# Sparse attention two heads deep: three logits tiles, mask added to the bias on GpSimd, late projections over ten heads

## The chip, the cores and the metric

One core of a Trainium2 chip. Its engines run their own queues in order and wait for each other through semaphores: TensorE (PE in the profile, its weight loads PEld) multiplies matrices into PSUM, VectorE (DVE) and ScalarE (ACT) read PSUM and SBUF, GpSimd (POOL) works on SBUF, and SyncE (SP) issues the DMAs. The metric is the device time of one execution in microseconds.

## The reference, cut to what matters

Two transformer layers over 512 tokens of width 1024. The first mixes tokens by stick-breaking attention, the second by sparse attention; after each comes a gated MLP with a short causal convolution. The change touches the second mixer alone:

```python
q = rms_norm(q.reshape(B, S, 16, 128), q_gain)      # 16 heads
k = rms_norm(lat, k_gain)                           # one shared latent key, 128 wide
isc = ...                                           # indexer scores, causal
_, sel = lax.top_k(isc, topk)                       # 128 keys kept for each query
logits = q . k[sel] * 128 ** -0.5 + rel_bias[bucket(t - sel)]
logits = where(sel <= t, logits, -1e30)
p = softmax(logits);  o = p @ lat[sel];  o = o @ w_uv   # per head
```

The kernel does not gather. It computes all causal logits and adds a mask, 0 for a kept key and -1e30 for another.

## The kernel before, in words

The order on every engine is the program's own order: the whole body is traced under a manual schedule, and tiles, buffers and semaphores are laid out by the framework. A tile name with `bufs=n` is a ring of n buffers; a new tile waits until the last reader of the old one in its buffer is done. Tags let several names share a ring.

The sparse attention (`dsa_layer`) first runs the indexer and the top-k. Under the top-k's VectorE work, eleven of the sixteen heads' queries are projected (`EARLY_Q = 11`): `project_steps` gives eight steps of three 512-column matmuls (`mm3`, high and low parts, L239 to L241). `q_hi` copies the result to `qh` and squares it into `q2`, `q_lo` forms the rest `ql`, `q_sum` sums the squares by eight tiny matmuls into PSUM tag "x", and `q_norm` turns sums into the scale `rq` (L916 to L920). Weight chunks (`raw`, six buffers, fetched by SP) are split into `whi` on ScalarE (L199) and `wlo` on VectorE (L207).

Then comes the edited part, the attention itself. A head has four query tiles j of 128 rows; tile j has (j + 1) x 128 causal keys, so a head has 1280 logits columns in a tile `L`. For each tile:

- `logits(h, j)`: on TensorE three matmuls of query parts with key parts into the PSUM tile z (tag "z", two buffers), and a fourth, L1106, that multiplies the identity with the mask `maskb` (bf16) and so adds the mask.
- `softmax(h, j)`: on VectorE L1114, z times the query's scale plus the bias, read backwards from `th`, into L; then L1116, the row maximum.
- `expo(h, j)`: on ScalarE the exponential in place (L1121), with its row sum.
- `transposed(h, pi)`: three groups of transposes of L on TensorE (4, 4 and 2 blocks, L1132; PSUM tag "tr", two buffers), each copied to `pT`.

For each pair of heads there are `pair_values` (values times latents, L1147), `weighted` (probabilities times values, sixteen matmuls, L1164), and the division by the row sums: `pair_sums` (copy `rvb`), `pair_scale` (transposes of `rvb` into `bc`), `pair_hi` and `pair_lo`. `load_bias(h)` is a DMA of 256 KB that writes the head's bias row, shifted by partition, into `th`.

In iteration h the loop transposes head h while it computes the logits of head h + 1. Four of the five late projections (heads 12 to 15) lie as filler in heads 1 to 8, four steps in each; the one of head 11 lies in the prologue, which computes head 0's logits. The last late head is finished in iteration 9, with one `q_norm(11, 16)`.

Of the kernel before, what the change touches and what calls it, by code (L numbers as in the profile page):

```python
# [9 lines left out]
F32 = mybir.dt.float32  # L10
# [8 lines left out]
D = 1024  # L19
S = 512  # L20
P = 128
# [14 lines left out]
H2 = S // 2  # L36
QRING = 12
EARLY_Q = 11
AHEAD = 2
FETCH = 1  # L40
IDXFILL = [1, 1, 1, 0, 1, 1, 1, 1]
# [74 lines left out]
def kernel_body(ctx, tc, xT, wst, cst, smalls, crow, relb, onehot, outT):  # L116
# [13 lines left out]
    def ptile(shape, name, tag):  # L130
        return banks.tile(shape, F32, name=name, tag=tag, bufs=nbanks[tag])
# [736 lines left out]
    def dsa_layer(l, first, man):  # L868
        with ExitStack() as st:
# [15 lines left out]
            def project_steps(ps, ck):  # L885
                whi, wlo = ck
                for k in range(KT):
                    w = slice(k * P, (k + 1) * P)
                    mm3(ps, whi[:, w], wlo[:, w], hs[k][0], hs[k][1], k == 0, k == KT - 1)
                    yield  # L890

            def q_hi(h, pt):
                qh = pp.tile([P, S], F32R, name="qh", bufs=QRING)
                ql = pp.tile([P, S], F32R, name="ql", bufs=QRING)
                q2 = pp.tile([P, S], F32, name="q2")
                act.activation(qh, pt, AF.Copy)
                act.activation(q2, pt, AF.Square)
                Q[h] = (qh, ql)
                Q[h, 2] = q2

# [5 lines left out]
            def q_sum(h):  # L906
                q2 = Q.pop((h, 2))
                ssq = ptile([P, QT], "ssq", "x")
                for j in range(QT):
                    pe.matmul(ssq[:, j:j + 1], lhsT=q2[:, j * P:(j + 1) * P], rhs=ones1, start=True, stop=True)  # L910
                c = slice(h * QT, (h + 1) * QT)
                act.activation(msq[:, c], ssq, AF.Copy, scale=1.0 / P)

# [159 lines left out]
            with ExitStack() as sa:  # L1073
# [2 lines left out]
                uvc = chunk_raw(("uv",)).rearrange("p (a b) -> p a b", a=HEADS)  # L1076
                ths = {}
                heads = {}
                late = {}

                def late_q(h):
                    late["h"], late["pt"] = h, ptile([P, S], "pt_q", "mm")
                    late["steps"] = project_steps(late["pt"], chunk(("dq", h), 0))

                def load_bias(h):
                    th = ths[h] = ap.tile([P, S], F32, name="th", bufs=2)
                    ov = rb[h:h + 1, 0:1]
                    nc.sync.dma_start(th, bass.AP(tensor=ov.tensor, offset=ov.offset, ap=[[1, P], [1, S]]))

                def begin(h):  # L1090
                    L = ap.tile([P, LW], F32, name="L")
                    if h % 2 == 0:
                        rv = ap.tile([P, QT, 2], F32, name="rv", bufs=4)
                        heads["rv"] = rv
                    heads[h] = (L, ap.tile([P, QT], F32, name="nm"), ap.tile([P, QT], F32, name="sum"), heads["rv"], {})

                def logits(h, j):
                    qh, ql = Q[h]
                    ns = (j + 1) * P
                    qs = slice(j * P, ns)  # L1100
                    ls = slice(LOFF[j], LOFF[j] + ns)
                    z = heads[h][4][j] = ptile([P, S], "z", "z")
                    pe.matmul(z[:, :ns], lhsT=qh[:, qs], rhs=kph[:, :ns], start=True, stop=False)
                    pe.matmul(z[:, :ns], lhsT=ql[:, qs], rhs=kph[:, :ns], start=False, stop=False)
                    pe.matmul(z[:, :ns], lhsT=qh[:, qs], rhs=kpl[:, :ns], start=False, stop=False)
                    pe.matmul(z[:, :ns], lhsT=ident_b, rhs=maskb[:, ls], start=False, stop=True)  # L1106

                def softmax(h, j):
                    L, nm, sum_, rv, z = heads[h]
                    z = z.pop(j)  # L1110
                    ns = (j + 1) * P
                    ls = slice(LOFF[j], LOFF[j] + ns)
                    c = h * QT + j
                    dve.scalar_tensor_tensor(L[:, ls], z[:, :ns], rq[:, c:c + 1], ths[h][:, :ns][:, ::-1],  # L1114
                                             op0=OP.mult, op1=OP.add)
                    dve.tensor_reduce(nm[:, j:j + 1], L[:, ls], axis=AX.X, op=OP.max, negate=True)  # L1116

# [47 lines left out]
                                          rhs=ts[e][:, c:c + n], start=i == 0, stop=pi == 2)  # L1165

                def pair_sums(rv):
                    rvb = ap.tile([P, QT, 2, 64], F32, name="rvb", tag="bs")
                    dve.tensor_copy(rvb, rv[:, :, :, None].to_broadcast([P, QT, 2, 64]))
                    return rvb  # L1170

                pair = {}
# [1 line left out]
                def pair_scale(rvb):  # L1174

                    bc = ptile([P, S], "bc", "x")
                    for j in range(QT):
                        pe.transpose(bc[:, j * P:(j + 1) * P], rvb[:, j].rearrange("p a b -> p (a b)"), ident)
                    bs = pair["bs"] = ap.tile([P, S], F32, name="bs")
                    act.activation(bs, bc, AF.Copy)  # L1180

                def pair_hi():
# [7 lines left out]
                def pair_lo():  # L1190
                    dve.tensor_sub(O[-1][1], pair["bs"], O[-1][0].bitcast(F32))

                load_bias(0)
                load_bias(1)
                begin(0)
                late_q(EARLY_Q)
                for j in range(QT):
                    logits(0, j)
                    drain(late["steps"], 2)
                    softmax(0, j)  # L1200
                    expo(0, j)
                    if j == 1:
                        split_hi()
                q_hi(late["h"], late["pt"])
                for h in range(HEADS):
                    n = h + 1
                    more = n < HEADS
                    filling = 1 <= h <= 2 * (HEADS - EARLY_Q - 1)
                    after = h > 1 and h % 2 and late["h"]
                    values = h % 2 == 0 and h > 0  # L1210
                    if more:
                        begin(n)
                        for j in range(2):
                            logits(n, j)
                        softmax(n, 0)
                        expo(n, 0)
                    if values:
                        weighted(h - 2)
                    transposed(h, 0, True)
                    if more:  # L1220
                        softmax(n, 1)
                        expo(n, 1)
                    if h == 0 or after:
                        q_lo(late["h"], late["pt"])
                    if after:
                        split_hi()
                        done = late["h"]
                        if not filling:
                            q_sum(done)
                    if h % 2 and h > 1:  # L1230
                        pair_lo()
                    if filling:
                        if h % 2:
                            late_q(EARLY_Q + 1 + h // 2)
                        drain(late["steps"], 2)
                    if more:
                        logits(n, 2)
                        softmax(n, 2)
                        expo(n, 2)
                    dve.reciprocal(heads[h][3][:, :, h % 2], heads[h][2])  # L1240
                    if values:
                        rvb = pair_sums(heads[h - 1][3])
                    transposed(h, 1, False)
                    if more:
                        logits(n, 3)
                    if h % 2:
                        pair_values(h - 1)
                    transposed(h, 2, True)
                    if values:
                        pair_scale(rvb)  # L1250
                    if more:
                        softmax(n, 3)
                        expo(n, 3)
                        if n + 1 < HEADS:
                            load_bias(n + 1)
                    if h == 0:
                        split_lo()
                    if h == 1:
                        split_hi()
                        split_lo()  # L1260
                        q_sum(EARLY_Q)
                    if after:
                        split_lo()
                        if filling:
                            q_sum(done)
                        else:
                            q_norm(EARLY_Q, HEADS)
                            late["h"] = None
                    if filling:
                        drain(late["steps"], 2)  # L1270
                        if h % 2 == 0:
                            q_hi(late["h"], late["pt"])
                    if values:
                        pair_hi()
                pair_scale(pair_sums(heads[HEADS - 1][3]))
# [113 lines left out]
```

## Time and profile before

| what | value |
|---|---|
| median of 3 runs | 1334.76 us (1333.66 to 1335.91) |
| profiled execution | 1335.43 us, its span 1333.7 us |
| mean granted clock of TensorE | 0.992 of 2.4 GHz |
| busy, share of the span | PE 96%, DVE 72%, ACT 44%, POOL 2% |
| attention part that is edited | 779.70 to 917.37 us of the span |

The span goes from the first instruction to the last; the run's time has a little around it. Busy shares are averages over stages with different limits, and a busy PE is not PE at its peak, since matmuls are pipelined and their ends are modelled. What a stage is worth is read from the stage itself: by stretch, by waits, and by the start times of neighbours on one queue.

### The profile page before, as it was taken

Reading aid. Unit: us, or ns where it says so; the run is one execution under the profiler, and the core shown is the slowest. Engines: PE = TensorE matmul, PEld = TensorE weight load, DVE = VectorE, ACT = ScalarE, POOL = GpSimd, SP = SyncE. Lnnn points to the kernel's source line nnn. Section 1 sums busy time; section 2 is a strip of 40 time slices with the busy share of each in tenths; the row PEclk is TensorE's granted clock in tenths of the full one; section 3 lists DMA queues with packets and bytes.
Section 4 is the critical chain, followed back from the end, with each engine's and each line's share of the span. In section 5 each row is a group of like instructions: output and inputs, shape, how many; then the busy total and the mean of one; then the engine's idle time right before and its main releaser. Section 6 shows DMA issues by size and latency. Waiting matters only on the chain.

```text
span 1333.7 us, 17868 instructions
## 1 busy us (share of the span) xinstructions
PE 1283.2 (96%) x6900; PEld 1069.2 (80%) x6900; DVE 960.9 (72%) x1570; ACT 592.3 (44%) x1051; POOL 22.9 (2%) x22
## 2 busy tenths in 40 slices
PE   2899999999999999999999999989999999999998
PEld 0688878799888888888988877766998888888888
DVE  6987988877877877875778986685676546556653
ACT  4575666454423323443554345573454324324430
POOL 3200000000000000000100000000000000000000
PEclk8999999999999999999999999999999999999999
DMA  7624343423566575554212211112222332333221
GB/s 276 242 82 159 117 146 121 143 75 103 182 227 199 179 244 192 190 180 153 77 51 79 79 48 61 59 41 110 72 87 76 114 105 77 108 106 95 72 87 64
DMA packets 49894, 162.69 MB, mean 122 GB/s; under 512 B 5601, under 2 KB 7905, under 8 KB 49810
## 3 DMA queue, kind: packets, MB, share of 16 engines
q1 hardware_dynamic: 49810, 161.56, 37.5%
q8 instruction: 54, 0.88, 0.3%
q14 instruction: 30, 0.25, 0.1%
HBM read 159.40 MB, written 2.14 MB: 121 GB/s over the span
## 4 chain that ended last, share of the span: by engine, by line
PE 89%; DVE 7%; ACT 2%; issue 1%; DMA 1%; SPq 0%; DVEq 0%; ACTq 0%
PE pt_u L240 11%; PE pt_u L239 11%; PE pt_u L241 11%; PE pt_d L240 5%; PE pt_d L241 5%; PE pt_d L239 5%; PE pt_q L239 2%; PE pt_q L241 2%; PE pt_q L240 2%; PE pt_l L239 2%; PE pt_l L240 2%; PE pt_l L241 2%; PE pt_first L241 2%; PE pt_first L239 2%; PE pt_qk L239 2%; PE pt_first L240 2%
## 5 line engine op out<-in xcount | busy, mean ns | idle before, releaser
L199 ACT ACTIVATE whi<-raw 128x1024 fp32r<-128x1024 f32 (+1 forms) x206 | 205.0, 1002 | 141.2 <-PE pt_d L241 102.6
L207 DVE TENSOR_TENSOR wlo<-raw,whi 128x1024 fp32r<-128x1024 f32 (+1 forms) x206 | 240.1, 1168 | 17.0 <-ACT whi L199 15.9
L240 PE MATMUL pt_u<-hhi,wlo 128*128 128x512 f32 x640 | 249.2, 389 | 0.0
L241 PE MATMUL pt_u<-hlo,whi 128*128 128x512 f32 x640 | 249.2, 389 | 0.0
L239 PE MATMUL pt_u<-hhi,whi 128*128 128x512 f32 x640 | 249.2, 389 | 0.0
L806 ACT ACTIVATE y<-pt_u,sm 128x512 f32<-128x512 f32 x80 | 62.1, 776 | 190.9 <-PE pt_u L241 190.9
L239 PEld LDWEIGHTS pt_u<-hhi,whi 128*128 128x128 f32 x640 | 120.1, 188 | 25.1
L241 PEld LDWEIGHTS pt_u<-hlo,whi 128*128 128x128 f32 x640 | 120.2, 188 | 24.8
L240 PEld LDWEIGHTS pt_u<-hhi,wlo 128*128 128x128 f32 x640 | 120.2, 188 | 24.7
L807 DVE SCALAR_TENSOR_TENSOR y<-pt_u,sm,y 128x511 f32<-128x511 f32 x80 | 59.9, 749 | 98.3 <-ACT y L806 98.3
L248 DVE SCALAR_TENSOR_TENSOR raw<-raw,cond 128x1024 f32<-128x1024 f32 x96 | 120.0, 1261 | 0.0
L241 PE MATMUL pt_d<-actlo,whi 128*128 128x512 f32 x288 | 112.2, 389 | 0.0
L239 PE MATMUL pt_d<-acthi,whi 128*128 128x512 f32 x288 | 112.1, 389 | 0.0
L240 PE MATMUL pt_d<-acthi,wlo 128*128 128x512 f32 x288 | 112.1, 389 | 0.0
L350 DVE SCALAR_TENSOR_TENSOR x<-pt_d,mod,x 128x512 f32<-128x512 f32 x48 | 36.0, 750 | 72.8 <-PE pt_d L241 72.8
L239 PE MATMUL pt_first<-hhi,whi 128*128 128x256 f32 (+1 forms) x224 | 69.4, 310 | 7.6 <-ACT hhi L532 7.6
L241 PE MATMUL pt_first<-hlo,whi 128*128 128x256 f32 (+1 forms) x224 | 68.8, 307 | 8.2 <-DVE hlo L535 7.9
L223 ACT ACTIVATE acthi<-y 128x512 fp32r<-128x512 f32 x44 | 27.8, 632 | 104.3 <-DVE y L825 104.3
L240 PE MATMUL pt_first<-hhi,wlo 128*128 128x256 f32 (+1 forms) x224 | 67.9, 303 | 0.0
L239 PEld LDWEIGHTS pt_d<-acthi,whi 128*128 128x128 f32 x288 | 54.1, 188 | 11.3
L240 PEld LDWEIGHTS pt_d<-acthi,wlo 128*128 128x128 f32 x288 | 54.1, 188 | 11.2
L241 PEld LDWEIGHTS pt_d<-actlo,whi 128*128 128x128 f32 x288 | 54.1, 188 | 11.2
(228 smaller groups left out, 2647.2 us busy)
## 6 DMA issues: line engine op xcount, KB each, us to landing
raw<-wst SPq DMA_DIRECT2D x255, 512.0 KB, 3.7
raw<-wst SPq DMA_DIRECT2D x48, 384.0 KB, 2.9
th<-rb SPq DMA_DIRECT2D x16, 256.0 KB, 3.2
x<-xT SPq DMA_DIRECT2D x8, 256.0 KB, 5.6
outT<-x SPq DMA_DIRECT2D x16, 128.0 KB, 1.7
sm<-smalls SPq DMA_DIRECT2D x1, 248.0 KB, 2.7
cons<-cst SPq DMA_DIRECT2D x1, 192.0 KB, 5.4
oh<-onehot SPq DMA_DIRECT2D x1, 80.0 KB, 1.8
```

The source lines that it names most:

```text
L199: act.activation(hi[:, :n], raw[:, :n], AF.Copy)
L207: dve.tensor_sub(lo[:, :n], raw[:, :n], hi[:, :n].bitcast(F32))
L223: act.activation(hi, src, AF.Copy)
L239: pe.matmul(out, lhsT=whi, rhs=ahi, start=start, stop=False)
L240: pe.matmul(out, lhsT=wlo, rhs=ahi, start=False, stop=False)
L241: pe.matmul(out, lhsT=whi, rhs=alo, start=False, stop=stop)
L248: dve.scalar_tensor_tensor(raw, raw, 1.0, cond, op0=OP.mult, op1=OP.mult, accum_out=dst)
L350: dve.scalar_tensor_tensor(x[f][:, c], pt, mod[l][:, g * KT + f:g * KT + f + 1], x[f][:, c], op0=OP.mult, op1=OP.add)
L806: act.activation(y, pt, AF.Identity, scale=cw[2], bias=sm[:, b + S_CB + c:b + S_CB + c + 1])
L807: dve.scalar_tensor_tensor(y[:, 1:], pt[:, :S - 1], cw[1], y[:, 1:], op0=OP.mult, op1=OP.add)
```

## The change

The mask no longer goes through TensorE: L1106 is removed, and `begin(h)` adds bias (read backwards) and mask into L on GpSimd, four adds a head. `softmax` then adds L to the scaled logits in place. There are three L tiles, and the loop works two heads ahead: iteration h transposes head h and computes the logits of head h + 2; the prologue computes heads 0 and 1. The adds for head h + 3 and the bias load for head h + 4 stand at the end of iteration h. `th` goes from two buffers to one; heads 1 and 2 take buffers of the weight ring.

The late projections are issued through `late_steps(n)`: two steps at each of the prologue's eight tiles, then one step at two places of every iteration and at a third place of every even one, until head 15 is done; that is 16 steps in the prologue and 24 in iterations 0 to 9. They are normalized in two groups, `q_norm(11, 14)` and `q_norm(14, 16)`.

To make room, `q2` and `rvb` become two half-size tiles each in rings of the norm (`ln`, `sqt`), written by two instructions for one; `bs` has one buffer. Within an iteration `weighted` and the first group of transposes now stand ahead of the second logits tile, and the second group of transposes ahead of the third.

```diff
...
 EARLY_Q = 11
+LATE_NORM = 14
...
         def q_hi(h, pt):
-        q2 = pp.tile([P, S], F32, name="q2")
+        q2 = [npool.tile([P, H2], F32, name="q2", tag="ln", bufs=2) for _ in range(2)]
         act.activation(qh, pt, AF.Copy)
-        act.activation(q2, pt, AF.Square)
+        for i in range(2):
+            act.activation(q2[i], pt[:, halves[i]], AF.Square)
...
         for j in range(QT):
-            pe.matmul(ssq[:, j:j + 1], lhsT=q2[:, j * P:(j + 1) * P], rhs=ones1, start=True, stop=True)
+            pe.matmul(ssq[:, j:j + 1], lhsT=q2[j // 2][:, j % 2 * P:j % 2 * P + P], rhs=ones1, start=True, stop=True)
...
         heads = {}
-        late = {}
-
-        def late_q(h):
-            late["h"], late["pt"] = h, ptile([P, S], "pt_q", "mm")
-            late["steps"] = project_steps(late["pt"], chunk(("dq", h), 0))
+        late = {"h": EARLY_Q, "k": 0, "done": []}
+
+        def late_steps(n):
+
+            for _ in range(n):
+                h = late["h"]
+                if h == HEADS:
+                    return
+                if late["k"] == 0:
+                    late["pt"] = ptile([P, S], "pt_q", "mm")
+                    late["steps"] = project_steps(late["pt"], chunk(("dq", h), 0))
+                next(late["steps"])
+                late["k"] += 1
+                if late["k"] == KT:
+                    drain(late["steps"])
+                    q_hi(h, late["pt"])
+                    late["done"].append((h, late["pt"]))
+                    late["k"] = 0
+                    late["h"] += 1
         def load_bias(h):
-            th = ths[h] = ap.tile([P, S], F32, name="th", bufs=2)
+            if h in (1, 2):
+                th = ths[h] = raws.tile([P, D], F32, name="th", tag="raw")[:, :S]
+            else:
+                th = ths[h] = ap.tile([P, S], F32, name="th", bufs=1)
             ov = rb[h:h + 1, 0:1]
             nc.sync.dma_start(th, bass.AP(tensor=ov.tensor, offset=ov.offset, ap=[[1, P], [1, S]]))
         def begin(h):
-            L = ap.tile([P, LW], F32, name="L")
+            L = ap.tile([P, LW], F32, name="L", bufs=3)
             if h % 2 == 0:
                 rv = ap.tile([P, QT, 2], F32, name="rv", bufs=4)
                 heads["rv"] = rv
-            heads[h] = (L, ap.tile([P, QT], F32, name="nm"), ap.tile([P, QT], F32, name="sum"), heads["rv"], {})
+            for j in range(QT):
+                ls = slice(LOFF[j], LOFF[j] + (j + 1) * P)
+                pool.tensor_add(L[:, ls], ths[h][:, :(j + 1) * P][:, ::-1], maskb[:, ls])
+            heads[h] = (L, ap.tile([P, QT], F32, name="nm", bufs=3), ap.tile([P, QT], F32, name="sum", bufs=3), heads["rv"], {})
...
         def logits(h, j):
-            ls = slice(LOFF[j], LOFF[j] + ns)
             z = heads[h][4][j] = ptile([P, S], "z", "z")
             pe.matmul(z[:, :ns], lhsT=qh[:, qs], rhs=kph[:, :ns], start=True, stop=False)
             pe.matmul(z[:, :ns], lhsT=ql[:, qs], rhs=kph[:, :ns], start=False, stop=False)
-            pe.matmul(z[:, :ns], lhsT=qh[:, qs], rhs=kpl[:, :ns], start=False, stop=False)
-            pe.matmul(z[:, :ns], lhsT=ident_b, rhs=maskb[:, ls], start=False, stop=True)
+            pe.matmul(z[:, :ns], lhsT=qh[:, qs], rhs=kpl[:, :ns], start=False, stop=True)
...
         def softmax(h, j):
-            dve.scalar_tensor_tensor(L[:, ls], z[:, :ns], rq[:, c:c + 1], ths[h][:, :ns][:, ::-1],
+            dve.scalar_tensor_tensor(L[:, ls], z[:, :ns], rq[:, c:c + 1], L[:, ls],
...
         def pair_sums(rv):
-            rvb = ap.tile([P, QT, 2, 64], F32, name="rvb", tag="bs")
-            dve.tensor_copy(rvb, rv[:, :, :, None].to_broadcast([P, QT, 2, 64]))
+            rvb = [npool.tile([P, H2], F32, name="rvb", tag="sqt", bufs=3) for _ in range(2)]
+            for i in range(2):
+                dve.tensor_copy(rvb[i].rearrange("p (a b c) -> p a b c", a=2, b=2),
+                                rv[:, 2 * i:2 * i + 2, :, None].to_broadcast([P, 2, 2, 64]))
...
             for j in range(QT):
-                pe.transpose(bc[:, j * P:(j + 1) * P], rvb[:, j].rearrange("p a b -> p (a b)"), ident)
-            bs = pair["bs"] = ap.tile([P, S], F32, name="bs")
+                pe.transpose(bc[:, j * P:(j + 1) * P], rvb[j // 2][:, j % 2 * P:j % 2 * P + P], ident)
+            bs = pair["bs"] = ap.tile([P, S], F32, name="bs", bufs=1)
...
-        load_bias(0)
-        load_bias(1)
-        begin(0)
-        late_q(EARLY_Q)
-        for j in range(QT):
-            logits(0, j)
-            drain(late["steps"], 2)
-            softmax(0, j)
-            expo(0, j)
-            if j == 1:
-                split_hi()
-        q_hi(late["h"], late["pt"])
+        for h in range(3):
+            load_bias(h)
+        for h in range(3):
+            begin(h)
+        load_bias(3)
+        for h in range(2):
+            for j in range(QT):
+                logits(h, j)
+                late_steps(2)
+                softmax(h, j)
+                expo(h, j)
+                if j == 1:
+                    split_hi()
+                if j == 2:
+                    split_lo()
+                if h == 1 and j == 0:
+                    q_lo(*late["done"][0])
+                if h == 1 and j == 2:
+                    q_sum(late["done"].pop(0)[0])
         for h in range(HEADS):
-            n = h + 1
+            n = h + 2
             more = n < HEADS
-            filling = 1 <= h <= 2 * (HEADS - EARLY_Q - 1)
-            after = h > 1 and h % 2 and late["h"]
             values = h % 2 == 0 and h > 0
+            done = late["done"].pop() if late["done"] else None
             if more:
-                begin(n)
-                for j in range(2):
-                    logits(n, j)
-                softmax(n, 0)
-                expo(n, 0)
+                logits(n, 0)
+            late_steps(1)
...
             if more:
+                softmax(n, 0)
+                expo(n, 0)
+                logits(n, 1)
                 softmax(n, 1)
                 expo(n, 1)
-            if h == 0 or after:
-                q_lo(late["h"], late["pt"])
-            if after:
+            if done:
+                q_lo(*done)
                 split_hi()
-                done = late["h"]
-                if not filling:
-                    q_sum(done)
             if h % 2 and h > 1:
                 pair_lo()
-            if filling:
-                if h % 2:
-                    late_q(EARLY_Q + 1 + h // 2)
-                drain(late["steps"], 2)
+            transposed(h, 1, False)
+            late_steps(1)
...
                 rvb = pair_sums(heads[h - 1][3])
-            transposed(h, 1, False)
+            transposed(h, 2, True)
...
                 pair_values(h - 1)
-            transposed(h, 2, True)
             if values:
                 pair_scale(rvb)
+            if done:
+                q_sum(done[0])
             if more:
                 softmax(n, 3)
                 expo(n, 3)
-                if n + 1 < HEADS:
-                    load_bias(n + 1)
-            if h == 0:
+            if done:
                 split_lo()
-            if h == 1:
-                split_hi()
-                split_lo()
-                q_sum(EARLY_Q)
-            if after:
-                split_lo()
-                if filling:
-                    q_sum(done)
-                else:
-                    q_norm(EARLY_Q, HEADS)
-                    late["h"] = None
-            if filling:
-                drain(late["steps"], 2)
-                if h % 2 == 0:
-                    q_hi(late["h"], late["pt"])
+                if done[0] == LATE_NORM - 1:
+                    q_norm(EARLY_Q, LATE_NORM)
+                elif done[0] == HEADS - 1:
+                    q_norm(LATE_NORM, HEADS)
+            if h + 3 < HEADS:
+                begin(h + 3)
+            if h + 4 < HEADS:
+                load_bias(h + 4)
+            if h % 2 == 0:
+                late_steps(1)
             if values:
                 pair_hi()
         pair_scale(pair_sums(heads[HEADS - 1][3]))
```

## Rows read from the trace of the kernel before

**Rows 1.** The profile's page: busy us, share of the span, instructions.

```profile
PE 1283.2 (96%) x6900; PEld 1069.2 (80%) x6900; DVE 960.9 (72%) x1570; ACT 592.3 (44%) x1051; POOL 22.9 (2%) x22
```

**Rows 2.** Stretch and length; PE, PEld, DVE, ACT, POOL busy; PEclk, DMA, GB/s.

```profile
779.70:789.41 9.71, 9.71 (x42) 7.76 (x42) 6.27 (x15) 5.59 (x12) 0.00 (x0) 0.82 0.18 57
844.62:863.20 18.58, 17.94 (x114) 13.83 (x114) 12.42 (x25) 10.35 (x28) 0.00 (x0) 1.00 0.19 56
893.11:906.19 13.08, 11.89 (x82) 8.51 (x82) 10.51 (x23) 8.08 (x24) 0.00 (x0) 1.00 0.52 180
779.70:917.37 137.67, 127.43 (x803) 95.79 (x802) 97.19 (x204) 82.24 (x220) 0.00 (x0) 0.99 0.22 70
```

**Rows 3.** Waits, 775 to 925 us: us in total, times, longest.

```profile
DVE L L1114 <- PE z L1106: 29.5, 17, 4.0
...
PE ssq L910 <- ACT vals L1151: 2.1, 4, 0.5
```

**Rows 4.** Timeline of DVE: start, us, what, idle time before it.

```profile
901.21 0.55 DVE L1116 TENSOR_REDUCE nm<-L 128x1 f32<-128x384 f32 x1
...
901.77 0.66 DVE L1139 COPY pT<-tr 128x512 f32<-128x512 f32 x1
902.34 0.74 DVE L1114 SCALAR_TENSOR_TENSOR L<-z,cols,th 128x512 f32<-128x512 f32 x1
...
904.30 0.47 DVE L1114 SCALAR_TENSOR_TENSOR L<-z,cols,th 128x256 f32<-128x256 f32 x1
...
907.51 0.62 DVE L1114 SCALAR_TENSOR_TENSOR L<-z,cols,th 128x384 f32<-128x384 f32 x1 [2.28 <-PE z L1106]
```

**Rows 5.** Timeline of PE around a first and second logits tile.

```profile
813.99 0.23 PE L1106 MATMUL z<-maskb,ident_b 128*128 128x128 bf16 x1
814.02 0.36 PE L1103 MATMUL z<-kph,qh 128*128 128x256 f32 x1
```

**Rows 6.** Timeline of PE in the late heads and at the end.

```profile
886.54 0.34 PE L1106 MATMUL z<-maskb,ident_b 128*128 128x384 bf16 x1
886.72 0.60 PE L1132 MATMUL tr<-cons,L 128*128 128x128 f32 x4
...
887.86 0.39 PE L1106 MATMUL z<-maskb,ident_b 128*128 128x512 bf16 x1
888.08 1.05 PE L1147 MATMUL pv<-raw,latf 128*128 128x128 f32 x8
...
890.74 2.38 PE L1164 MATMUL av<-pT,vals 128*64 128x512 f32 x16
893.04 0.66 PE L1132 MATMUL tr<-cons,L 128*128 128x128 f32 x4
893.45 0.42 PE L1103 MATMUL z<-kph,qh 128*128 128x384 f32 x1
...
912.00 0.77 PE L1132 MATMUL tr<-cons,L 128*128 128x128 f32 x5 [1.68 <-ACT L L1121]
```

**Rows 7.** Timeline of all engines around the late norm.

```profile
875.83 0.69 DVE L1116 TENSOR_REDUCE nm<-L 128x1 f32<-128x512 f32 x1
...
876.44 1.21 DVE L207 TENSOR_TENSOR wlo<-raw,whi 128x1024 fp32r<-128x1024 f32 x1
...
877.39 1.28 ACT L916 ACT_TABLE_LOAD   x1
...
879.95 0.35 DVE L1114 SCALAR_TENSOR_TENSOR L<-z,cols,th 128x128 f32<-128x128 f32 x1
```

**Rows 8.** Line L525 on POOL: count, duration ns min/median/max, first and last start.

```profile
L525 POOL TENSOR_TENSOR xr<-x,r x8: 1260/2238/2253, 22.0 to 35.8; 128x512 f32<-128x512 f32 x8
```

**Rows 9.** Timeline of DVE in the first layer's start.

```profile
36.88 2.28 DVE L248 SCALAR_TENSOR_TENSOR raw<-raw,cond 128x1024 f32<-128x1024 f32 x1
...
39.90 1.21 DVE L248 SCALAR_TENSOR_TENSOR raw<-raw,cond 128x1024 f32<-128x1024 f32 x1
```

**Rows 10.** Tile th: its DMAs from issue to landing.

```profile
DMA to landing us min/median/max: 3.0/3.2/4.6
```


## Prediction

> **What bounds the kernel now.** I read the profile from the outside in. The page first: TensorE (PE) is busy 96% of the span and GpSimd (POOL) 2% [rows 1], so what shortens PE's own queue can pay, and what relieves another engine pays only where PE waits for it. Then busy time by stretch: the edited attention runs from 779.70 to 917.37 us, 137.67 us with PE busy 127.43, and it has two regimes [rows 2]. While late query projections fill PE (the pair of heads at 844.62) a pair takes 18.58 us, PE 17.94 of it, VectorE (DVE) 12.42: PE sets the pace. Behind the last projection (893.11) a pair takes 13.08 us with DVE busy 10.51. The waits say who is late: DVE sits 29.5 us before the softmax's first step (L1114) for the logits tile z, released by the mask matmul L1106 [rows 3]. In the late regime one wait is typical: 2.28 us at the third tile [rows 4], whose logits stand on PE behind `weighted`. Without it DVE's work in such a pair is 13.08 - 2.28 = 10.8.
>
> **The sum's base.** The profiled execution took 1335.43 us (span 1333.7 plus 1.7 around it); the median of the three runs, 1334.76, lies 0.7 below. I work out the stretch in the trace and carry the difference to the median.
>
> **Mask matmuls: 64 leave PE.** What one costs is the step from its start to the start of what follows: 0.03 us for 128 columns [rows 5], 0.18 for 384 and 0.22 for 512 [rows 6]; 256 lies between, 0.12 as an estimate. That is 0.55 a head, 8.8 us in all, and counts fully only where PE sets the pace.
>
> **Ten filled heads.** A late step is three 512-column matmuls; at a little over the 0.22 of [rows 6] that is 0.69. A filled pair had eight; now 24 steps lie in heads 0 to 9 and 16 in the prologue: five a pair. A pair with a `q_sum` becomes 18.58 - 1.1 (mask) - 2.05 (three steps) = 15.4. One without also saves eight tiny matmuls (taken as pv's eight, 1.05 [rows 6]) and a wait of 0.5 for their bank [rows 3]: 13.9. Pair 0/1 has no `weighted` and no `bc` (3.0 less) but a `q_sum` (1.0): 11.9. So 11.9 + 15.4 + 13.9 + 15.4 + 13.2 (one step fewer) = 69.8 us. DVE has 10.9 a pair, plus 1.9 (a split, `ql`) where a projection ends: PE hides it.
>
> **Prologue.** 9.71 us now [rows 2]; minus 0.6 of mask, plus a second head: logits 1.9 (three matmuls a tile), eight steps 5.5, `q_sum` 1.05: 17.6. The first softmax now waits for bias load and add in a row. Behind it stand all of DVE and, after two tiles, PE. The wait is one quarter's add (0.4, below); two z buffers and four steps cover it. On SP's queue the fourth bias load waits for POOL's first four adds, until some 787, and the next weight fetch stands behind it; its chunk is split only in head 0, near 800: nothing.
>
> **Heads 10 to 13.** The change goes two heads deep, but z still has two buffers. Once DVE has read the third z tile of an odd head, it has that tile's reduce and the reciprocal, 0.56, then the fourth tile and the next head's first, 1.96 [rows 4]: 2.5 us. PE meanwhile needs logits 0.35, `weighted` 2.3, four transposes 0.4 [rows 6], logits 0.35 and 0.1 of hand-over: 3.5. DVE idles 1.0 instead of 2.28; a pair takes 13.08 - 1.3 + 0.1 (two half `rvb` copies for one) = 11.9, say 12.0. Head 10 also carries the last projection's `ql` (0.7, like the 0.74 of a same-sized step [rows 4]), its split (1.21) and its norm: from the reduce at 875.83 the next softmax comes only at 879.95, 4.1 us, of which reduce and split explain 1.8; a table load on ScalarE before its one step and another for the return to the exponential fill most of the rest [rows 7]. I charge 0.7 + 1.2 + 2.3, less 0.6 of DVE idle time: 3.6. The new first norm (head 3) has the same price, but PE there has 7 us of work (pv, sums, `weighted`, steps) before it needs that DVE: nothing; bare, 2.3 to 3.5. Sum 12.0 + 3.6 + 12.0 = 27.6.
>
> **Heads 14, 15, end.** PE work and copies: `weighted` twice 4.6, 20 transposes 2.0, pv 0.9, two `bc` 0.8, and about the present end's wait (1.68 [rows 6]), 1.5: 9.8.
>
> Together 17.6 + 69.8 + 27.6 + 9.8 = 124.8 against 137.67: 12.9 less if POOL costs nothing.
>
> **POOL's adds.** 64 adds, 1280 columns a head. The nearest row is POOL's multiply of 512 columns in the first layer: 1.26 us at best, 2.24 as a rule [rows 8]; here one operand is bf16 and one is read backwards, which no row shows. At 2.46 ns a column a head costs 3.2 us, at 4.4 ns 5.6. I take 3.2, since the long ones ran beside a DVE full of two-input work. An add starts when the head three before has been transposed (its L buffer), some 2 us before DVE wants the first quarter, which needs 0.3 to 0.6: hidden. So late it stalls DVE, and the `pT` copies behind, for which PE's transposes wait.
>
> The long times are mutual: a DVE operation on 1024 columns with both inputs in SBUF took 2.28 us beside POOL and 1.21 once POOL had finished [rows 9]. The Trainium skill (SBUF — State Buffer, "Who interferes with whom") says why: VectorE's second read port is GpSimd's, locked for a whole instruction by VectorE operations with two SBUF inputs or in a two-port mode, not by those with one SBUF input. By that rule the softmax step (z is in PSUM) and its reduce run freely beside POOL; if every DVE operation locked, the adds would cost what rival (a) assumes. No row shows POOL beside such a softmax.
>
> I therefore charge the splits, `olo`, the `rvb` copies and the norm's small steps: some ten in heads 10 to 13, where DVE sets the pace, with POOL busy 3.2 of every 6 us and 0.4 us of an add left: 10 x 0.5 x 0.4 = 2.0, and 0.5 elsewhere. From below 0 (never met); from above a whole pass of adds in three heads, 9.7. I take 2.5.
>
> Halved q2: one more ScalarE instruction a head; ScalarE is busy 82 of the 137.67 us [rows 2]: nothing; bare, 0.2 once, at the end of the top-k loop.
>
> **Forecast.** 124.8 + 2.5 = 127.3, 10.4 less: 1334.76 - 10.4 = 1324.4.
>
> **Rivals.** (a) *The bias loop sets the pace: slower.* `th` has one buffer, so a row load starts when POOL has read the last one, and POOL starts when it has landed, 3.2 us later [rows 10]. The period is adds + 3.2 + 0.3. At adds of 3.2 it is 6.7 us, under the filled heads' 7, and slack covers the three tail heads. At 5.6 it is 9.1: adds for head 3 start near 801.3, those for head 15 twelve periods later, 910.5; its third quarter is ready 3.9 later, and 9.8 to the end: 924.2, 6.8 later than now: 1341.6. It loses time from a period of some 8.6 (adds over 5.1, 4 ns a column) and eats the gain from 7.8. For it: the long multiplies; against: few lockers in this stretch.
> (b) *DVE stays the brake.* The unfilled pairs keep 13.08 (+2.2) and lock waits double (+2.5): 5.7 gained, 1329.1. For it: two z buffers; against: one tile fewer stands behind `weighted`.
> (c) *Given back.* The mask's 8.8 are won, the first norm is bare (3.5) and lock waits reach 5.0; the balance of the steps brings nothing: 1334.5. Against: PE's 7 us of cover.
>
> **Chances.** Forecast (7 to 14 off) 0.58; (b) (2.7 to 7 off) 0.19; (c) 0.09; (a) 0.14. No change can be told within about 0.2% (2.7 us). Faster 0.77, same 0.09, slower 0.14. The range goes to 1320, where POOL locks cost nothing and waits shrink, and up to 1336, over (b) and (c); most of (a) is left out.
>
> **What would show it.** No L1106; POOL some 51 us busier, with 512-column adds near 1.26; filled pairs at 13.9 to 15.4, unfilled ones at 12; DVE's 29.5 us for z more than halved. I am wrong if DVE waits for POOL head after head, if the 512-column add is over 2 us, or if POOL itself waits for `th`.

## The result: slower by 13 us

The changed kernel takes 1348.1 us (median of 4 runs, 1348.06 to 1348.73) against 1335.34 for the kernel before beside it: ratio 1.0097, 95% interval 1.0084 to 1.0111. The forecast was 1324.4, with a range from 1320 to 1336; it is wrong in sign and in range.

First the page of the changed kernel:

```profile
span 1346.2 us, 17898 instructions
...
PE 1283.2 (95%) x6836; PEld 1070.5 (80%) x6836; DVE 968.3 (72%) x1582; ACT 596.7 (44%) x1070; POOL 73.5 (5%) x86
```

The 64 mask matmuls are gone and POOL has 50.6 us more, as forecast. Yet PE is busy exactly as long as in [rows 1]. Fewer matmuls took as long, so some of them ran slower. The stretches, with the columns of [rows 2]: the prologue, the filled pair of heads 6 and 7, the unfilled pair 12 and 13, the whole attention:

```profile
779.02:796.56 17.54, 17.54 (x83) 14.70 (x83) 13.62 (x28) 10.26 (x25) 10.17 (x12) 0.90 0.40 120
842.99:861.60 18.61, 15.10 (x98) 11.63 (x97) 14.77 (x30) 11.83 (x33) 8.18 (x10) 0.99 0.23 62
901.40:917.17 15.77, 11.27 (x74) 8.19 (x73) 12.38 (x25) 8.55 (x27) 3.65 (x5) 0.97 0.44 151
779.02:929.87 150.85, 127.64 (x739) 97.23 (x738) 104.94 (x218) 86.00 (x228) 50.65 (x64) 0.91 0.20 63
```

The loss sits here: 150.85 against 137.67, 13.2 us more, where the whole span grew by 12.5. The prologue came out as worked out (17.6). The filled pair has 15.10 of PE work, near the forecast pace, but 3.5 us in which PE stands idle. Over the whole stretch PE idles 23.2 us where it idled 10.2 [rows 2], at a granted clock of 0.91 where it had 0.99. The waits from 775 to 945 us:

```profile
...
POOL L L1116 <- PE tr L1152: 65.7, 11, 11.1
DVE L L1134 <- PE z L1126: 25.3, 16, 6.1
...
PE bc L1200 <- DVE rvb L1190: 10.1, 12, 2.7
...
PE ssq L912 <- ACT vals L1171: 4.2, 2, 2.1
```

DVE's wait for the logits is hardly less than the 29.5 of [rows 3], and PE has two new waits: for the copied row sums, and for the bank of `q_sum`, whose longest was 0.5 in [rows 3]. POOL waits for others; DVE waited for POOL once, 1.4 us, in the prologue. The groups by shape show at which tile DVE waits (mean ns behind the busy time, then its idle time before), and what an add costs:

```profile
L1190 DVE COPY rvb<-rv 128x256 f32<-128x256 f32 x16 | 8.9, 597 | 0.0
...
L1134 DVE SCALAR_TENSOR_TENSOR L<-z,cols,L 128x256 f32<-128x256 f32 x16 | 7.7, 482 | 22.4 <-PE z L1126 22.3
```

```profile
L1116 POOL TENSOR_TENSOR L<-th,maskb 128x512 f32<-128x512 f32 x16 | 18.9, 1182 | 0.0
```

22.3 of DVE's wait falls at the second tile, which in even heads now stands behind `weighted`. How that reaches PE is read from the timeline of all engines in heads 6 and 7:

```profile
844.47 2.37 PE L1184 MATMUL av<-pT,vals 128*64 128x512 f32 x16 [0.20 <-ACT vals L1171]
...
847.90 0.48 DVE L1134 SCALAR_TENSOR_TENSOR L<-z,cols,L 128x256 f32<-128x256 f32 x1 [2.74 <-PE z L1126]
...
850.78 1.19 DVE L1190 COPY rvb<-rv 128x256 f32<-128x256 f32 x2
...
851.10 0.44 PE L1200 MATMUL bc<-cons,rvb 128*128 128x128 f32 x2 [0.72 <-DVE rvb L1190]
...
852.02 0.44 PE L1200 MATMUL bc<-cons,rvb 128*128 128x128 f32 x2 [0.49 <-DVE rvb L1190]
...
858.98 0.62 ACT L1141 ACTIVATE L<-L,nm 128x384 f32<-128x384 f32 x1 [1.36 <-DVE nm L1136]
...
859.86 0.64 ACT L1171 ACTIVATE vals<-pv 128x256 f32<-128x256 f32 x2
...
860.56 1.19 PE L912 MATMUL ssq<-ecols,q 128*128 128x1 f32 x8 [2.10 <-ACT vals L1171]
```

Even head: PE runs `weighted`, DVE waits 2.74 for the tile behind it, and so comes late through tiles two and three to the reciprocal and `rvb`. PE has meanwhile issued the fourth tile's logits, and what is next in its queue is `bc`, which needs `rvb`: idle 0.72, and 0.49 once more for the second half. Odd head: next in PE's queue behind `pair_values` stands `q_sum`, which needs the PSUM bank that `vals` is copied out of; that copy stands on ScalarE behind the third tile's exponential, which waits for DVE's maximum: idle 2.10. In head 10 both kinds of wait come at one pair, for `vals` ahead of `weighted` and for `rvb` ahead of `bc`:

```profile
881.15 2.37 PE L1184 MATMUL av<-pT,vals 128*64 128x512 f32 x16 [1.10 <-ACT vals L1171]
...
889.04 1.11 PE L1200 MATMUL bc<-cons,rvb 128*128 128x128 f32 x4 [2.69 <-DVE rvb L1190]
```

What follows on PE shows in the windows around both waits before `q_sum` (heads 3 and 7) and behind the one of 2.69 us:

```profile
820.00:830.00 10.00, 7.91 (x43) 5.46 (x43) 7.08 (x16) 7.01 (x18) 3.14 (x4) 0.86 0.29 91
860.00:870.00 10.00, 9.44 (x44) 5.84 (x44) 2.76 (x6) 2.36 (x8) 0.15 (x1) 0.66 0.10 26
890.00:900.00 10.00, 8.13 (x32) 7.16 (x32) 6.17 (x15) 6.30 (x13) 1.10 (x3) 0.50 0.08 23
```

And in PE's timeline behind the wait of 2.10:

```profile
863.80 4.51 PE L1184 MATMUL av<-pT,vals 128*64 128x512 f32 x16
```

After these idle stretches the granted clock is at 1.2 GHz for a while (0.50 is that level alone, the values between mix the two), and the same sixteen matmuls of `weighted` take 4.51 us where they took 2.37.

### The profile page after: what moved, and what is told of

Read it like the earlier page. It is cut to its first block, busy times and chain, and to the rows that moved or that the text cites. A ratio compares the mean times of both kernels' runs of the same rounds, so it can differ in the third digit from the quotient of the medians.

```text
span 1346.2 us, 17898 instructions
## 1 busy us (share of the span) xinstructions
PE 1283.2 (95%) x6836; PEld 1070.5 (80%) x6836; DVE 968.3 (72%) x1582; ACT 596.7 (44%) x1070; POOL 73.5 (5%) x86
## 4 chain that ended last, share of the span: by engine, by line
PE 89%; DVE 7%; ACT 2%; issue 1%; DMA 1%; SPq 0%; DVEq 0%; ACTq 0%
PE pt_u L241 11%; PE pt_u L240 11%; PE pt_u L242 11%; PE pt_d L240 5%; PE pt_d L241 5%; PE pt_d L242 5%; PE pt_q L240 2%; PE pt_q L242 2%; PE pt_q L241 2%; PE pt_l L240 2%; PE pt_l L241 2%; PE pt_l L242 2%; PE pt_first L242 2%; PE pt_first L240 2%; PE pt_qk L240 2%; PE pt_first L241 2%
## 5 line engine op out<-in xcount | busy, mean ns | idle before, releaser
L208 DVE TENSOR_TENSOR wlo<-raw,whi 128x1024 fp32r<-128x1024 f32 (+1 forms) x206 | 240.7, 1171 | 15.3 <-ACT whi L200 14.3
```

Of the source, the lines that this page charges most:

```text
L208: dve.tensor_sub(lo[:, :n], raw[:, :n], hi[:, :n].bitcast(F32))
```

## The experiments

Each is an edit of the changed kernel unless said otherwise, with a median beside runs of the kernel before on the same chip (1336.37 for e1 to e4, 1335.54 for e5 to e8, 1336.41 for e9 to e12). The theory: PE is blocked by instructions whose producer on DVE or ScalarE is late, since the second tile went behind `weighted`, and the clock then multiplies the loss. The rival: the adds on GpSimd lock DVE.

**e1: the second tile's logits ahead of `weighted`.**

```diff
                     late_steps(1)
+                    if more:
+                        logits(n, 1)
                     if values:
                         weighted(h - 2)
...
-                        logits(n, 1)
                         softmax(n, 1)
```

> Edit: the second logits tile goes back in front of weighted on PE. Theory order (weighted ahead of the second tile starves DVE by 2.7 us in every even head, so DVE is late at rvb and PE then waits for it at bc): DVE's longest wait for z falls below 1.5 us, PE's wait at bc halves, 1348 becomes 1338 to 1342. Theory lock (GpSimd's adds stretch the rvb copies and PE waits at bc for that alone): within 3 us of 1348, wait at bc unchanged near 10 us. Theory bank (the waits of 2.1 us at q_sum and the halved clock behind them are the loss): within 3 us of 1348.

1344.88 us, ratio 1.0061 (1.0046 to 1.0076), in none of the three ranges expected. DVE's wait for z falls from 25.3 to 5.4 us in all, the longest 0.7, but PE still waits 7.5 us for `rvb` and 1.65 and 1.66 before `q_sum`, with the granted clock at 0.87 and 0.83 in 820 to 830 and 860 to 870. The late tile alone is not the loss.

**e2: `rvb` copied at the start of the iteration.**

```diff
+                    if values:
+                        rvb = pair_sums(heads[h - 1][3])
                     if more:
                         logits(n, 0)
...
-                    if values:
-                        rvb = pair_sums(heads[h - 1][3])
                     transposed(h, 2, True)
```

> Edit: the rvb copies stand at the top of the iteration on DVE, before the first tile of the head two ahead. Theory order: rvb is no longer late, the 10.1 us of PE at bc nearly vanish, but DVE still starves: 1340 to 1343. Theory lock: the copies fall outside the adds and go back to about 0.25 us each, and the wait at bc vanishes: 1336 to 1340. Theory bank: PE gains the wait at bc of the even heads but keeps both waits of 2.1 us at q_sum: 1342 to 1346.

1337.7 us, ratio 1.0008 (0.9998 to 1.0017). The time lies in the range expected of the lock, but its reason did not come: a half `rvb` still takes 427 ns. PE's wait for `rvb` is gone all the same, so it was the copies' place in DVE's queue, more than their length, that made PE wait. The waits of `q_sum` (1.76 and 2.13) stay, and with them a clock of 0.80 and 0.83 in those two windows.

**e3: no adds on GpSimd.**

```diff
-                    for j in range(QT):
-                        ls = slice(LOFF[j], LOFF[j] + (j + 1) * P)
-                        pool.tensor_add(L[:, ls], ths[h][:, :(j + 1) * P][:, ::-1], maskb[:, ls])
...
-rq[:, c:c + 1], L[:, ls],
+rq[:, c:c + 1], latf[:, :ns],
```

> Edit: GpSimd's adds are left out, so bias and mask are not in the logits (another resident tile is added in their place, of the same shape); all else as in the changed kernel. Theory lock: rvb copies return to some 0.25 us each, the wait at bc falls from 10 to about 4 us, 1348 becomes 1338 to 1342. Theory order: DVE's 2.7 us for z and most of the wait at bc stay, 1344 to 1347. Theory bank: both 2.1 us waits stay, 1344 to 1348.

This run leaves the bias and the mask out of the logits and adds another tile of the same shape, for its time alone. 1340.74 us, ratio 1.0033 (1.002 to 1.0046), in the range expected of the lock, but still slower than before without a single add. `q_sum` waits 2.02, and the clock in 820 to 830 is 0.68. But the adds are not free: without them `rvb` takes 277 ns a half for 597, and PE's wait for it is 5.7 us for 10.1.

```profile
L1187 DVE COPY rvb<-rv 128x256 f32<-128x256 f32 x16 | 3.7, 277 | 0.0
```

So the rival explains a part, by way of the wait in which it falls. Most of that part is the clock: the stretch is 9.5 us shorter (141.32), of which 3.2 are idle time of PE and 6.3 are PE work that ran faster.

**e4: `q_sum` ahead of `pair_values`.**

```diff
                     transposed(h, 1, False)
+                    if done:
+                        q_sum(done[0])
                     late_steps(1)
...
-                    if done:
-                        q_sum(done[0])
```

> Edit: q_sum's tiny matmuls stand behind the second group of transposes, ahead of pair_values, so they do not wait for the copy of vals out of the same PSUM bank. Theory bank: the two waits of 2.1 us vanish and so does the halved clock behind them (weighted back at 2.37 us in heads 4 and 8): 1348 becomes 1338 to 1341. Theory order or lock: 4 us of waiting go, 1343 to 1345, if the clock still falls elsewhere.

1338.97 us, ratio 1.0021 (1.0012 to 1.0031). The windows:

```profile
820.00:830.00 10.00, 10.00 (x73) 7.87 (x72) 8.34 (x20) 8.63 (x23) 3.08 (x4) 1.00 0.37 103
860.00:870.00 10.00, 8.49 (x57) 6.60 (x53) 7.99 (x18) 6.01 (x17) 3.18 (x4) 1.00 0.21 53
```

With the two waits gone the clock is full in both, and 73 matmul records fit where there were 43. Behind a later wait of 1.67 us it still falls, to 0.50 in 885 to 890. This is the test of the clock's part: two waits of 4.2 us together were worth 0.76% of the time, some 10 us. The stretch took 141.05 us with PE busy 121.26, so of the 9.8 us that it lost 3.4 were idle time and 6.4 slow matmuls.

**e6 (e2 and e4) and e5 (e1, e2 and e4).**

> Both earlier edits together: rvb copies at the top of the iteration, q_sum ahead of pair_values. If in-order waits of PE behind late DVE and ScalarE work are the whole loss, and each edit removes its own (10.4 and 9.1 us alone), the sum is 1348.1 - 19.5 = 1328 to 1331, with no stretch under full clock except at the late norm. If each alone already removed the same halved clock, they overlap: 1333 to 1337. Theory lock: rvb copies at 0.28 us when clear of the adds, 0.4 to 0.6 when not, and the splits still at 1.35.

> As the run with both, and the second logits tile ahead of weighted as well. Theory order: DVE no longer sits 2.7 us in even heads, another 2 to 4 us go: 1326 to 1329. If PE sets the pace once its waits are gone, DVE's idle time there costs nothing and the tile's wait for a z buffer may add some: within 1.5 us of the run with both.

e6: 1329.74 us, ratio 0.9954 (0.9939 to 0.9969). e5: 1326.61 us (1325.2 to 1328.12), ratio 0.9929 (0.9914 to 0.9944). The stretches of e5: prologue, heads 6 and 7, heads 10 and 11, and the whole:

```profile
779.38:796.91 17.53, 17.53 (x82) 14.70 (x82) 13.61 (x28) 10.27 (x25) 10.17 (x12) 0.90 0.37 120
837.13:851.61 14.48, 14.47 (x97) 11.63 (x97) 12.62 (x28) 10.09 (x30) 6.43 (x10) 1.00 0.26 74
865.36:882.32 16.96, 13.12 (x84) 10.21 (x82) 15.13 (x31) 12.40 (x32) 7.89 (x11) 0.90 0.20 62
779.38:907.90 128.52, 117.90 (x739) 93.16 (x738) 104.64 (x218) 84.40 (x228) 50.34 (x64) 0.97 0.24 74
```

The same 739 matmul records now take 117.90 us for 127.64. Of the 22.3 us between the two stretches 9.7 are matmuls that no longer run slowly and 12.6 are idle time of PE. In points of the ratio (0.01 each), e1, e2 and e4 alone bring 0.36, 0.89 and 0.76, in sum 2.01, and all three together 1.68: most of it adds up.

**e7: e5 with the norm's VectorE steps behind the next head's reciprocal**, to take them out of PE's one long wait that is left in e5, at the late norm (PE's timeline of e5):

```profile
878.17 0.44 PE L1124 MATMUL z<-kph,qh 128*128 128x384 f32 x1 [3.34 <-DVE L L1134]
```

```diff
-                            q_norm(EARLY_Q, LATE_NORM)
+                            norm_rsqrt(EARLY_Q, LATE_NORM)
+                            late["norm"] = (EARLY_Q, LATE_NORM)
...
                     dve.reciprocal(heads[h][3][:, :, h % 2], heads[h][2])
+                    if "norm" in late:
+                        norm_steps(*late.pop("norm"))
```

> As the run with all three, and the late norm in two pieces: ScalarE's reciprocal root where it was, DVE's four steps one head later, behind that head's third tile. If DVE's wait for the root (3.6 us at 895.33 in the changed kernel) and PE's wait behind it are on the path, 2 to 4 us less than with all three, 1324 to 1327; if ScalarE's two table loads hold the exponentials anyway, the same time.

A miss: 1329.44 us, ratio 0.9954 (0.9939 to 0.9968), 2.8 above e5. Its timeline, POOL's line first and then DVE's:

```profile
830.05 3.09 POOL L1123 TENSOR_TENSOR L<-th,maskb 128x128 f32<-128x128 f32 x4 [4.65 <-PE tr L1159]
```

```profile
831.18 0.86 DVE L927 SCALAR_TENSOR_TENSOR cols<-cols 128x12 f32<-128x12 f32 x1
832.08 1.09 DVE L928 SCALAR_TENSOR_TENSOR cols<-cols 128x12 f32<-128x12 f32 x1
833.20 0.17 DVE L929 TENSOR_SCALAR cols<-cols 128x12 f32<-128x12 f32 x1
```

The same two steps in e5, of which this is the first, by shape, where they meet no add:

```profile
L920 DVE SCALAR_TENSOR_TENSOR cols<-cols 128x12 f32<-128x12 f32 x1 | 0.2, 170 | 0.0
```

The steps were moved into the adds: twelve columns take 0.86 and 1.09 us for 0.17, and all of DVE waits behind them. They end at 832.04 and 833.17, where the adds of 384 and 512 columns end (begun at 831.1 and 832.0, of 0.94 and 1.18 us). The Trainium skill (SBUF — State Buffer, "Who interferes with whom") says that a VectorE instruction with two SBUF inputs contends with a GpSimd instruction that reads SBUF, and that the port pair they share is an exclusive lock. The trace agrees: each slow step lasted until an add was over.

The move did bring something where it was aimed: heads 10 and 11 took 15.3 us for 17.0 in e5. It lost 1.75 in heads 4 and 5, where the steps of the first norm met the adds, and 3.6 in heads 12 and 13, where those of the second met them and `weighted` took 4.05 us for 2.37 behind a wait of 1.72.

**e8: e6 with the mask matmul back on PE**, GpSimd only copying the reversed bias.

```diff
-pool.tensor_add(L[:, ls], ths[h][:, :(j + 1) * P][:, ::-1], maskb[:, ls])
+pool.tensor_copy(L[:, ls], ths[h][:, :(j + 1) * P][:, ::-1])
...
-                    pe.matmul(z[:, :ns], lhsT=qh[:, qs], rhs=kpl[:, :ns], start=False, stop=True)
+                    pe.matmul(z[:, :ns], lhsT=qh[:, qs], rhs=kpl[:, :ns], start=False, stop=False)
+                    pe.matmul(z[:, :ns], lhsT=ident_b, rhs=maskb[:, LOFF[j]:LOFF[j] + ns], start=False, stop=True)
```

> As the run with both, but the mask goes through PE again (the 64 matmuls are back) and GpSimd only copies the reversed bias into L. If PE sets the pace after the two edits, the mask is worth what the prediction said and this is 6 to 9 us slower than the run with both; if DVE or ScalarE sets it, 0 to 4 us slower.

1334.18 us, ratio 0.9986 (0.9977 to 0.9996), 4.4 above e6, between the two ranges expected. That is what taking the mask from PE is worth net of what the adds cost more than copies: beside the copies a half `rvb` takes 286 ns (413 in e6).

**e9: e5 with e3's edit (no adds).**

> The run with all three edits, with GpSimd's adds left out, so bias and mask are not in the logits (another resident tile of the same shape is added). It prices the lock once PE is not blocked otherwise. If the lock costs what the prediction charged, 2.5 us less than with all three, 1323 to 1325; if it is only carried by waits that the three edits removed, under 1 us; if splits and the norm's small steps carry it on the path, 4 to 6 us less, 1321 to 1323.

As in e3, bias and mask are left out. 1326.65 us, ratio 0.9927 (0.9913 to 0.994); e5 repeated beside it as e12 took 1327.46. The two are not told apart, and their stretches differ by 0.6 us (127.80 and 128.39). Once PE no longer waits for `rvb`, nor for `vals` before `q_sum`, the adds cost 0.8 us by the medians; the intervals do not exclude nothing, nor the 2.5 that the prediction charged.

**e10: the kernel before, with the same two moves as in e6** (`pair_sums` to the start of the iteration, `q_sum` ahead of `pair_values`).

```diff
+                    if values:
+                        rvb = pair_sums(heads[h - 1][3])
                     if more:
                         begin(n)
...
-                        if not filling:
-                            q_sum(done)
+                        q_sum(done)
...
-                    if values:
-                        rvb = pair_sums(heads[h - 1][3])
...
-                        if filling:
-                            q_sum(done)
-                        else:
+                        if not filling:
```

> The kernel before with the same two edits (rvb copies at the top of the iteration, q_sum ahead of pair_values). If the edits are worth their 18 us only because the change made PE wait there, the kernel before gains what it loses there now, 0.35 us at each of seven bc and 0.5 at each of four q_sum, 2 to 4 us: 1331.5 to 1333.5. If the edits are the whole gain and depth and mask bring nothing, it comes down to 1327 to 1329.

1333.96 us, ratio 0.9988 (0.9979 to 0.9997), 2.4 below the kernel before and 0.5 above the range expected. The moves are worth 2.4 there and 1.43 points of the ratio, some 19 us, in the changed kernel: the waits that they take away are made by the new order. With the moves, the change itself brings 6.5 (1327.46 in e12 against 1333.96); e12's third move only gives the second tile the place ahead of `weighted` that it has in the kernel before.

**e11 and e12: e5 with `weighted` behind the first transposes in head 14, and e5 again.**

```diff
-                    if values:
+                    if values and more:
                         weighted(h - 2)
                     transposed(h, 0, True)
+                    if values and not more:
+                        weighted(h - 2)
```

> The run with all three edits, and in head 14 weighted stands behind the first group of transposes, so that PE has work while ScalarE copies vals (PE waits 1.84 us there). If that wait is on the path: 1 to 2 us less than with all three. If the copies of the transposes behind it only wait instead: no change.

> The kernel with all three edits once more, beside its variants on one chip: 1325 to 1328, and under the kernel before by 8 to 10 us.

e11: 1325.24 us, ratio 0.9924 (0.9912 to 0.9937); e12: 1327.46 us, 0.9936 (0.9923 to 0.9948). PE's wait for `vals` falls from 1.85 to 1.40, but the 2.2 between the two lie within their intervals. e5 and e11 beat both kernels, by 0.6 to 0.8% against before.

## Why the prediction was wrong

**What bounds, and the prologue: right.** PE's queue held the time; in e5 it is busy 14.47 of the 14.48 us of heads 6 and 7. The prologue took 17.54 us for 17.6, with PE busy throughout: the wait for the first add was 1.4 us for a quarter's 0.4 and cost nothing.

**Mask matmuls: the count right, the worth mis-sized.** 64 matmuls went; 8.8 was worked out for all of them, of which the sum takes off 6.1 (1.1 in each of five filled pairs, 0.6 in the prologue). Measured were 4.4, net, in e8.

**Ten filled heads: the failed step is "PE hides it".** The sum counted DVE's work (10.9 a pair, and 1.9) against PE's and took the smaller as hidden. Hidden is a matter of order, not of sums. In heads 6 and 7 DVE had 14.77 busy in 18.61, so there was time; but PE's queue holds `bc` and `q_sum` at fixed places, and both need a product that DVE or ScalarE makes late. The five pairs took 11.2, 18.7, 16.6, 18.6 and 17.9 us for 11.9, 15.4, 13.9, 15.4 and 13.2. In e5, with only the order of three blocks changed, they took 11.95, 14.96, 13.31, 14.48 and 13.75: within 1 us, the terms were right for a PE that isn't blocked. The prediction had taken `q_sum`'s bank wait at the old 0.5; behind `pair_values` it was 2.1 in heads 3 and 7.

**Heads 10 to 13: "DVE idles 1.0 instead of 2.28" failed.** DVE waits 2.74 in head 10 and 2.60 in head 12, no less than in [rows 4], only at the second tile in place of the third. In head 10 DVE's work beside it was credited rightly, 2.6 for 2.5; PE's 3.5 was not. Its logits began 0.3 us later than assumed, behind `pair_values`, and took 5.1 us to the second tile, since `weighted` waited 1.10 for the copy of `vals`, a wait that the sum puts at nothing. The effect of DVE's wait on `rvb`, and of `rvb` on PE, was not followed: heads 10 and 11 took 21.9 for 15.6, with PE's wait of 2.69 for `rvb` and a clock of 0.50 behind it, and heads 12 and 13 took 15.8 for 12.0.

**Heads 14, 15, end: mis-sized.** 12.7 us were measured for 9.8, 12.2 in e5. PE's work was 9.6 for 8.3, and its waits 3.1 for 1.5.

**A term that was missing: the clock.** It had 0.99 in the old stretch, and the prediction took every PE duration at that level. In the changed kernel the same matmuls take 9.7 us more than in e5. e4 shows where it comes from: two waits gone, the clock full behind them, 6.4 us less of PE work.

**POOL's adds: the mechanism right, the charge mis-sized and in the wrong place.** An add costs what was taken (50.65 us in 16 heads, 3.2 a head, and 1.18 for the 512 columns). `rvb` is lengthened, so are the splits (1.71 us in e5 for 1.22 in e3) and in e7 the norm's steps, while the softmax step is not (0.73 at 512 columns, 0.74 in [rows 4]). Charged were 2.5 us. Where `rvb` is on PE's path it was more: e3 stands 0.64 points of the ratio, some 8.5 us, below the changed kernel, most of it by way of the clock. Where it isn't, 0.8 us (e9), not told apart from nothing.

**The rivals.** (a) gave the sign but not the cause: its period needs adds of over 5.1 us a head, and DVE waited for POOL once, 1.4 us, while POOL waited 65.7 for transposes. (b) came nearest, in that DVE's wait for z stayed; its price of 4.7 on the forecast missed what follows on PE. (c) is not what happened: its 1334.5 is a gain given back, and the loss came from waits that it does not hold. The cause was no rival at all. The whole stretch in e5 is 128.5 us for a forecast 127.3, and its time 1326.6 for 1324.4: the forecast nearly holds for a kernel in which PE's queue is not blocked, though in part by luck. The filled pairs came out at 68.4 for 69.8; from head 10 on it is 42.5 for 37.4 and most of the 2.5 for the adds: 17.0 for 15.6 (with the wait of 3.34 at the late norm), 13.4 for 12.0, and 12.2 for 9.8 at the end.

**Open.** Whether another place for the norm's steps, clear of the adds, brings the 3.34 back was not tried, nor were three z buffers. Why the clock falls behind one wait and not behind another of the same length is not shown.

## What to carry to other kernels

When a software pipeline goes deeper, walk through each in-order queue and ask of every instruction that waits on another engine what its producer stands behind; "the sum of the other engine's work is smaller" hides nothing. Keep small cross-engine steps (row sums, bank hand-overs) early, and keep two tiles of input for the next engine ahead of a long block. And price an idle stretch of TensorE by the matmuls behind it too, in rows taken at the lower clock.

## What the runs showed of the hardware

- Behind idle stretches of PE of 2.1 to 2.7 us the granted clock fell to its 1.2 GHz level, and in e1 and e2 behind one of 1.65 and one of 1.76; `weighted` then took up to 4.51 us for 2.37.
- The length of a wait alone does not tell it. In e3 PE waits 2.02 us before `q_sum` twice: behind the first, which ends at 823.12, the clock is 0.50 in 825 to 830; behind the second, which ends at 858.06, it is 1.00 from 860 to 870. The wait of 1.68 in [rows 6] was not followed by a fall either.
- A VectorE step on twelve columns with two SBUF inputs took 0.86 and 1.09 us beside GpSimd's adds (e7) and 0.17 alone (e5); the two long ones ended when an add did.
- A GpSimd add with a bf16 operand and one read backwards took 1.18 us for 512 columns, no more than the f32 multiply's best of 1.26 [rows 8]; a copy there, with one input, took 0.62 and left VectorE's `rvb` at 286 ns (e8).
